# Retention in written order with lags, resident tiles refilled through their low part, and attention rows gated where they are made

## The chip, the cores and the metric

The kernel runs on one core of one Trainium2 chip. The metric is the device time of one execution in microseconds. The kernel before took 2122.32 us (median of 3 runs, 2121.36 to 2124.02). The core has five engines with a queue each: TensorE (PE in the profile, its weight loads PEld), VectorE (DVE), ScalarE (ACT), GpSimd (POOL) and SyncE (SP). In this kernel nearly all DMAs are issued by SP, one after the other.

## What is computed

One layer of a streaming encoder on 2048 rows of 1024 numbers, in float32. The rows are normalised and projected to 8192 columns, which are split into the queries, keys, values and gate of a chunked attention (8 heads of 64), the same for a retention (8 heads, keys of 64, values of 128), and two merge gates:

```python
h = rms_norm(x, norm_gain[l])
proj = jnp.einsum('bsd,df->bsf', h, w_in[l])
q_a, k_a, v_a, g_a, q_r, k_r, v_r, g_r, m_a, m_r = split_columns(proj)
o_a = chunk_band_attention(q_a, k_a, v_a, rel_bias[l])     # heads reshaped
branch_a = einsum(o_a * silu(g_a), w_out_attn[l])
o_r = retention_chunkwise(rotary(q_r), rotary(k_r), v_r, gn_gain[l])
branch_r = einsum(o_r * silu(g_r), w_out_ret[l])
mixed = sigmoid(m_a) * branch_a + sigmoid(m_r) * branch_r
x = x + einsum(mixed, w_out[l])
return rms_norm(x, final_gain)
```

Attention looks at a row's own chunk of 64 rows and the 8 before. Retention is a linear attention with a decay per head: within a block, masked scores times values; across blocks, a state of 64 x 128 per head that is carried on. Each head's output is divided by its own standard deviation (group norm), times a gain.

## The kernel before

**Numbers in two parts.** A float32 matrix is held as a high part, rounded to the type TensorE multiplies fast, and a low part, the rest. ACT makes the high part (`split`, `to_parts`: `act.copy`), DVE or POOL the low part by subtraction. A product is then three matmuls: high x high, high x low, low x high.

**The dense stream.** All large matrix products form one list, `seq`, of products in fixed order: `p0` and `g0` (projection of the first 1024 rows to queries, keys, values, then to gates), `p1` and `g1` (the same for the second 1024 rows), `ba0`, `br0`, `ba1`, `br1` (the two branch outputs of each half) and `out`. The jobs p and g run in chunks of 256 weight columns, each 7 products of Strassen's kind over 7 resident tiles `R[0..6]` (each with a high and a low part) that hold combinations of the normalised rows. The others are plain products over resident tiles that hold gated branch inputs (`ya`, `yr`) or `w_out`. One product is 12 matmuls of 512 columns in 4 steps of 3. p0, g0, p1 and g1 have 392 steps each, ba 64, br 128, out 256: 2208 steps. Weights (`raw`) are loaded one chunk ahead and made into parts 3 products ahead (`prime`, `prepare`).

**Steps as a clock of the program.** `step()` puts out one step of the stream. `later(n, fn)` puts `fn` out n steps later, `put(lag, ...)` is a store by DMA after that lag, `fill(n)` puts out n dense steps between pieces of attention or retention (fractions are kept as credit), and `limit` stops `fill` at a step. `hook` calls a function after a given product.

**Order of the queues.** TensorE and SP always run in the order in which the program is written. ACT, DVE and POOL do so while `strict[0]` is set (the projections); in attention, retention and merge a planner orders them by a model of cost. Each engine takes its queue in order, so that a waiting instruction holds those behind it.

**Stages.** p0; then `heads(0)`, which is attention of the first half with 1.0 steps of g0 at each place and retention with 2.7; p1; `heads(1)` with g1 and the first part of ba0 and br0, 1.25 and 3.3 steps; then the merge. Each stage has its pool `E` of 512-column tiles (22, 15, 21, 22 of them). Attention begins at step 412 of the stream and puts out 18 + 168 x 1.0 = 186 steps in the first half and 18 + 192 x 1.25 = 258 in the second; a retention has 12 + 69 fills.

**Retention** goes over 4 pairs of heads and 4 blocks of 256 rows (16 units), two heads each (32 items). `load` brings keys, queries, values and decayed keys of a unit (`kr`, `qr`, `vr`, `kd`) and is called some one and a half units ahead. `scores` makes `sr` in PSUM, two items ahead; DVE multiplies it by the decay mask, ACT and DVE make `sh` and `sl`. `update` makes `kv` and adds it to the state. `output` multiplies into the one PSUM bank `o`; `evacuate` copies it out (`oz`, ACT), stores it, squares it on POOL, splits the square, and one unit later `pend` sums it over rows with matmuls into `ssq`. At the end a chain of DVE instructions turns `ssq` into the reciprocal deviations `rrow`.

**Refills.** `reload` (after each product of g0's last chunk) loads the second half's combinations into tiles `hl` of `E` and splits them into `R`. `fill_ya` loads attention output and its gate, multiplies and splits; `finish_yr` (16 times in p1, 16 times in the merge) loads a head's retention output and gate, multiplies them with the gain, multiplies by the deviation, which a matmul `rb` with `rrow` spreads over partitions, and stores; `fill_yr` and `fill_wo` load and split. Line 135 of the profile is the helper that records an instruction in written order; lines 206 and 207 are `split`.

## Time and profile before

| | |
|---|---|
| median of 3 runs | 2122.32 us |
| profiled execution | 2128.98 us, span 2127.2 us |
| TensorE busy | 1972.2 us, 93%, 9744 matmuls |
| mean granted TensorE clock | 0.971 |
| attention, first and second half | from 383 to 625 us, from 1165 to 1485 us |
| retention, first and second half | from 625 to 862 us (with its chain), from 1485 to 1754 us |
| projections | from 0 to 383 us, from 862 to 1165 us |
| merge and output | from 1754 to 2127 us |

A row of waits names the instruction that waited, what released it, the total, how often and the longest. A row of a group gives line, engine, operation, output and inputs by the program's names, shape and count, then busy time, mean ns of one, and the idle time before with its releaser. A row of a tile gives least, median and greatest ns. The ends of matmuls are modelled, so that PE busy can run over short waits.

### The profile page before, as it was taken

The page shows a single profiled execution, that of the slowest core. Times are in us where ns is not written, and L with a number is a line of the kernel's source. Part 1 is how long each engine was busy: PE and PEld are TensorE (multiplying, and loading weights), DVE is VectorE, ACT ScalarE, POOL GpSimd, SP SyncE. Part 2 cuts the span into 40 slices and gives each one's busy share as a digit, 9 for nine tenths or more (in the row PEclk, how much of TensorE's full clock was granted, in tenths as well). Part 3 has the DMA queues.
Part 4 walks back from the last instruction along what each step waited for, and adds up shares of the span by engine and source line. Part 5 has one row for each costly group of instructions (what it writes and reads, how often), then busy time and mean ns, then how long its engine had stood idle before and what let it go on. Part 6 is the DMA issues. An engine that isn't in the chain of part 4 may idle for free. (4 is left out here: it accounts for less than half of the span.)

```text
span 2127.2 us, 30311 instructions
## 1 busy us (share of the span) xinstructions
PE 1972.2 (93%) x9744; PEld 1638.4 (77%) x9744; DVE 1426.2 (67%) x2491; ACT 873.3 (41%) x1727; POOL 794.2 (37%) x868
## 2 busy tenths in 40 slices
PE   5799899999999997899999999999989888999998
PEld 4677777888888886777787888888867776788886
DVE  6867777777757667778877666665665567444554
ACT  5344333556554445233334555555443230222221
POOL 2544764554433324244544544443330131021000
PEclk9899999999999998999999999999989989999999
DMA  5376786645447768566675544443879978986564
GB/s 158 91 249 180 216 274 201 203 138 154 155 139 246 232 212 275 185 222 202 201 250 185 173 153 135 147 143 100 239 245 320 296 249 317 332 294 218 192 191 142
DMA packets 335951, 438.94 MB, mean 206 GB/s; under 512 B 29976, under 2 KB 193456, under 8 KB 335792
## 3 DMA queue, kind: packets, MB, share of 16 engines
q1 hardware_dynamic: 334752, 436.99, 64.3%
q8 instruction: 78, 1.28, 0.3%
q14 instruction: 81, 0.66, 0.1%
q10 hardware_dynamic: 1040, 0.00, 0.0%
HBM read 286.13 MB, written 150.76 MB: 205 GB/s over the span
## 5 line engine op out<-in xcount | busy, mean ns | idle before, releaser
L1180 POOL TENSOR_SCALAR pr<-pr,rsum 128x640 f32<-128x640 f32 (+4 forms) x128 | 96.5, 754 | 192.9 <-DVE rsum L1179 156.1
L135 PE MATMUL ps_p_z<-r,wh_p 128*128 128x512 f32 x448 | 144.5, 404 | 13.2 <-DVE c_p L135 7.7
L135 PE MATMUL ps_p_x<-r,wh_p 128*128 128x512 f32 x448 | 145.2, 405 | 4.8 <-DVE r L135 4.7
L135 PE MATMUL ps_g_z<-r,wh_g 128*128 128x512 f32 x448 | 144.9, 405 | 1.8 <-DVE u_g L344 1.3
L135 PE MATMUL ps_g_x<-r,wh_g 128*128 128x512 f32 x448 | 146.4, 408 | 0.0
L1178 ACT ACTIVATE pr<-pr,mn 128x640 f32<-128x640 f32 (+4 forms) x128 | 97.7, 763 | 113.6 <-DVE mn L1175 113.2
L135 POOL TENSOR_TENSOR t_p<-raw_p,t_p 128x512 f32<-128x512 f32 x50 | 72.0, 1440 | 147.3 <-DVE wl_p L135 132.0
L207 DVE TENSOR_TENSOR ptl<-tp,pth 128x384 fp32r<-128x384 f32 x168 | 98.9, 598 | 34.3 <-ACT pth L206 31.8
L1065 POOL TENSOR_TENSOR gr<-gr,ta 128x512 f32<-128x512 f32 x32 | 47.1, 1473 | 194.0 <-DVE gr L1064 179.5
L1175 DVE CUSTOM_DVE_ANT_0 pr<-wide,bt 128x640 f32<-128x640 f32 (+4 forms) x128 | 94.2, 736 | 29.5 <-PE wide L135 28.2
L281 POOL TENSOR_TENSOR wl_g<-t_g,wh_g 128x512 fp32r<-128x512 f32 x52 | 67.5, 1297 | 118.2 <-ACT wh_g L280 114.3
L135 PEld LDWEIGHTS ps_p_z<-r,wh_p 128*128 128x128 f32 x448 | 84.1, 193 | 30.8 <-issue 14.4
L135 PEld LDWEIGHTS ps_p_x<-r,wh_p 128*128 128x128 f32 x448 | 85.3, 194 | 23.4 <-DVE r L135 5.7
L206 ACT CAST pth<-tp 128x384 fp32r<-128x384 f32 x168 | 84.1, 512 | 37.7 <-PE tp L135 33.1
L135 DVE TENSOR_TENSOR wl_p<-t_p,wh_p 128x512 fp32r<-128x512 f32 x108 | 98.7, 914 | 0.4 <-ACT wh_p L135 0.4
L135 PE MATMUL ps_p_x<-r,wl_p 128*128 128x512 f32 x224 | 90.2, 403 | 6.9 <-DVE wl_p L135 6.9
L1388 POOL TENSOR_TENSOR o<-oz 128x512 f32<-128x512 f32 x32 | 35.2, 1101 | 163.9 <-ACT oz L1381 142.9
L135 PEld LDWEIGHTS tp<-ident,pr 128*128 128x128 f32 x560 | 70.2, 140 | 33.8 <-DVE ptl L207 10.3
L135 PE MATMUL tp<-ident,pr 128*128 128x128 f32 x560 | 89.2, 273 | 7.0 <-DVE ptl L207 6.5
L135 PE MATMUL wide<-ka,qa 128*128 128x512 f32 (+2 forms) x448 | 93.9, 326 | 1.2 <-DVE mn L1175 1.2
L135 PE MATMUL ps_p_z<-r,wl_p 128*128 128x512 f32 x224 | 89.5, 399 | 0.4 <-DVE wl_p L135 0.4
L280 ACT CAST wh_g<-t_g 128x512 fp32r<-128x512 f32 x104 | 64.5, 621 | 61.2 <-PE ps_g_y L135 22.1
(1222 smaller groups left out, 5925.8 us busy)
## 6 DMA issues: line engine op xcount, KB each, us to landing
raw_g<-in_w_in_dram SPq DMA_DIRECT2D x56, 512.0 KB, 6.4
raw_p<-in_w_in_dram SPq DMA_DIRECT2D x52, 512.0 KB, 6.0
qa<-qas SPq DMA_DIRECT2D x128, 128.0 KB, 2.9
qr<-qrs SPq DMA_DIRECT2D x128, 128.0 KB, 3.7
vr<-vrs SPq DMA_DIRECT2D x64, 256.0 KB, 4.1
ka<-kas SPq DMA_DIRECT2D x40, 256.0 KB, 2.9
va<-vas SPq DMA_DIRECT2D x40, 256.0 KB, 3.2
kds<-kdt_k SPq DMA_DIRECT2D x32, 256.0 KB, 3.2
```

Of the source, the lines that this page charges most:

```text
L135: return tc.keep_in_program_order(op(*a, **k))
L206: act.copy(dst_h, src)
L207: (eng or dve).tensor_tensor(dst_l, src, r32(dst_h), ALU.subtract)
L280: act.copy(wh, src)
L281: soon(LO_LAG if strict[0] else 0, lambda: eng.tensor_tensor(wl, src, r32(wh), ALU.subtract))
L1065: pool.tensor_tensor(g, g, ta, ALU.add)
L1175: dve.tensor_tensor_reduce(pr[:, 0:w], sp, bts[h][:, WIN - w:WIN], 1.0, 3.0e38, ALU.add, ALU.min, mn,)
L1178: act.activation(pr[:, 0:w], pr[:, 0:w], AF.Exp, bias=mn, scale=-1.0, accum_out=rsum)
L1180: pool.tensor_scalar(pr[:, 0:w], pr[:, 0:w], rsum, 1.0, ALU.mult, ALU.mult)
L1388: pool.tensor_tensor(o2, oz, oz, ALU.mult)
```

## The change

**Retention.** All engines are put in written order after the first 12 steps (`strict[0]`), and stay so through p1. What was put out at once now has lags: scores, mask product (DVE, now into a tile `sm`), high part (ACT), low part (now POOL); `kv`, state additions, `sstk`; copy and square of `o` (the square now by ACT from PSUM), its high and low part (POOL). `sure` puts out what is deferred where an output needs it. `load` is cut in two, keys and queries two units ahead and values one unit ahead. 2.3 dense steps at each place instead of 2.7 and 3.3; attention 1.0 in both halves. In the first half `limit` keeps g0's last chunk (28 steps) out of the retention; it runs after it, with the pools of p1.

**Deviations.** The chain of 12 DVE instructions is spread over steps and its result is stored to memory (`rsscr`); `finish_yr` loads a row of it broadcast over 128 partitions and multiplies on POOL, without a matmul. In the merge the 16 calls start at step 14, every 8 steps, instead of 8 and 2.

**Refills.** `refill` loads float32 values straight into the low part of a resident tile, copies the high part from it, and subtracts in place; the lags are in steps. It stands in for tiles of `E` in `reload`, `fill_ya` and `fill_yr`; the first four calls of `fill_yr` move from ba0 to the end of g1, 14 steps apart. g0's last chunk takes its products in the order of p.

**Attention** loads the gate of a head and multiplies its output by it on POOL before storing, so that `fill_ya` loads one tile instead of two.

**Weights** are loaded 9 and 8 products before their chunk (`RAW_LEADS`) instead of 7, and in strict order the sums of the chunks of g are put out one by one. Every `E` pool has a tile more.

The diff, cut to its core:

```diff
-E_PROJ = 22
-E_ATT = 15
-E_RET = 21
-E_MRG = 22
+E_PROJ = 23
+E_ATT = 16
+E_RET = 22
+E_MRG = 23
...
-ATT_FILLS = (1.0, 1.25)
-RET_FILLS = (2.7, 3.3)
+ATT_FILLS = (1.0, 1.0)
+RET_FILLS = (2.3, 2.3)
+RAW_LEADS = (9, 8)
...
-YR_FROM = 8
-YR_EVERY = 2
+YR_FROM = 14
+YR_EVERY = 8
...
-    SUM_AT = {True: {0: ("t1", "t2"), 4: ("t3",), 2: ("t4",)}, False: {0: ("t1", "t2", "t3"), 3: ("t4",)}}
+    SUM_AT = {
+        "p": {0: ("t1", "t2"), 4: ("t3",), 2: ("t4",)},
+        "g": {0: ("t1", "t2"), 2: ("t3",), 5: ("t4",)},
+        "loose": {0: ("t1", "t2", "t3"), 3: ("t4",)},
+    }
...
-            seq = [(c, k) for c in range(n) for k in per]
+            self.orders = [name[0]] * n
+            if name == "g0":
+                self.orders[-1] = "p"
+            seq = [(c, k) for c in range(n) for k in (per if resident else ORDERS[self.orders[c]])]
...
-                if ch.job.name[0] == "p":
+                if isinstance(ch, Strassen):
                     ch.sums(k)
...
-        count = {}
+        count, begins = {}, {}
+        for at, (job, ch, n) in enumerate(seq):
+            if isinstance(ch, Strassen):
+                begins.setdefault(ch, at)
+        sooner = {at - lead: (ch, [j]) for ch, at in begins.items() for j, lead in enumerate(RAW_LEADS)}
         for at, (job, ch, n) in enumerate(seq):
             count[ch] = count.get(ch, 0) + 1
+            if at in sooner:
+                ch2, js = sooner[at]
+                if ch2.raw is None or js[0]:
+                    len(ch2.raw or ()) == js[0] and ch2.load(js)
             if count[ch] == job.when + 1 and ch in following and following[ch].raw is None:
                 following[ch].load()
...
-    def reload(m):
+    def refill(m, k, src, lag, low=None):
+        wh, wl = R[m][0][:, k, :], R[m][1][:, k, :]
+        dma(r32(wl), src)
+        later(lag, lambda: act.copy(wh, r32(wl)))
+        later(lag + 2, lambda: (low or dve).tensor_tensor(wl, r32(wl), r32(wh), ALU.subtract))
+    def reload(n):
+        m, at = PRODUCTS[n][0], ORDERS["p"].index(n)
         for k in range(4):
-            a = E(f"hl_{m}_{k}")
-            dma(a, cscr[m][k])
-            to_parts(m, k, a, pool if k == 3 else dve)
+            t = 4 * at + k
+            later(1, lambda k=k, t=t: refill(m, k, cscr[m][k], 7 + 4 * t // 3 - 4 * at, pool if t % 3 == 2 else dve))
...
     def fill_ya(s, i, m):
         for k in range(4):
-            b = 2 * s + i
-            a, u = E(f"ya_{k}_{b}"), E(f"yu_{k}_{b}")
-            dma(a, oascr[k][b])
-            dma(u, uascr[k][b])
-            (pool if k % 2 else dve).tensor_tensor(a, a, u, ALU.mult)
-            to_parts(m, k, a)
+            later(1 + k, lambda k=k: refill(m, k, oascr[k][2 * s + i], 8))
...
     def finish_yr(h, b, lead):
-        a, u = E(f"yr_{h}_{b}"), E(f"yv_{h}_{b}")
+        a, u, r = (E(f"{n}_{h}_{b}") for n in ("yr", "yv", "rb"))
         dma(a, orscr[h // 2][b][h % 2])
         dma(u, urscr[h][b])
-        row = NOH + 8 * b + h
+        dma(r, rsscr[b // 2][8 * b + h].rearrange("(o d) -> o d", o=1).broadcast_to([P, B]))
         def gated():
             dve.scalar_tensor_tensor(a, a, gn[:, h:h + 1], u, ALU.mult, ALU.mult)
         def rest():
-            rb = TR(f"rb_{h}_{b}")
-            pe.matmul(rb, ohr[:, row:row + 1].broadcast_to([P, P]), rrow, start=True, stop=True)
-            dve.tensor_tensor(a, rb, a, ALU.mult)
+            pool.tensor_tensor(a, a, r, ALU.mult)
             put(6, yrscr[h][b], a)
...
     def fill_yr(s, i, j, m):
         for k in range(4):
-            h, b = 4 * j + k, 2 * s + i
-            a = E(f"yq_{h}_{b}")
-            dma(a, yrscr[h][b])
-            to_parts(m, k, a)
+            later(1 + 2 * k, lambda k=k: refill(m, k, yrscr[4 * j + k][2 * s + i], 10))
...
     def fill_wo(i, j, m):
-        for k in range(4):
+        def fetch(k):
             a = E(f"wo_{i}_{j}_{k}")
             row = (4 * j + k) * P
             dma(a, w_out[0, row:row + P, 512 * i:512 * i + 512])
-            to_parts(m, k, a)
+            later(10, lambda: act.copy(R[m][0][:, k, :], a))
+            later(12, lambda: dve.tensor_tensor(R[m][1][:, k, :], a, r32(R[m][0][:, k, :]), ALU.subtract))
+        for k in range(4):
+            later(1 + 2 * k, lambda k=k: fetch(k))
...
                 oa = E(f"oa_{h}_{b}")[0:64]
                 act.copy(oa, po[64:128])
                 dve.tensor_tensor(oa, po[0:64], oa, ALU.add)
-                put(3, oascr[h // 2][b][64 * (h % 2):64 * (h % 2) + 64], oa)
+                pool.tensor_tensor(oa, oa, uts.pop((h, b)), ALU.mult)
+                put(6, oascr[h // 2][b][64 * (h % 2):64 * (h % 2) + 64], oa)
...
             if m < len(units):
                 prs[m].append(soft(h, b, un, 1))
+                if un == 1:
+                    load_u(h, b)
...
+        def load_valued(p, st):
+            b, un = st // 2, st % 2
+            nm = f"{p}_{st}"
+            kd = E(f"kd_{nm}", F32R, (P, 2, T))
+            dma(r32(kd), r32(kdscr[p][b][:, un]))
+            vs = []
+            for i in range(2):
...
-            dve.tensor_tensor(sp, sp, dms[p][i], ALU.mult)
-            sh = E(f"sh_{nm}", F32R)
-            sl = E(f"sl_{nm}", F32R)
-            split(sh, sl, sp)
-            return sh, sl
+            got = []
+            def masked():
+                sm = E(f"sm_{nm}")
+                dve.tensor_tensor(sm, sp, dms[p][i], ALU.mult)
+                later(2, lambda: high(sm))
+            def high(sm):
+                got.append(E(f"sh_{nm}", F32R))
+                act.copy(got[0], sm)
+                later(2, lambda: low(sm))
+            def low(sm):
+                got.append(E(f"sl_{nm}", F32R))
+                pool.tensor_tensor(got[1], sm, r32(got[0]), ALU.subtract)
+            later(1, masked)
+            return got
...
+            def added():
...
+                sstk = epool[0].tile([P, 2, DV], F32R, tag="sstk", bufs=2, name=f"sstk_{p}_{st}")
+                sstks[p, st + 1] = sstk
+                later(3, lambda: high(sstk))
+            def high(sstk):
+                act.copy(sstk[0:64], state)
+                later(1, lambda: low(sstk))
+            def low(sstk):
+                dve.tensor_tensor(sstk[64:128], state, r32(sstk[0:64]), ALU.subtract)
+                if st == 3:
...
+            later(1, added)
+        def sure(here):
+            while not here():
+                deferred.pop(0)[2]()
         def output(p, st, i, parts, ops):
-            _, qs, vs, _ = tiles[p, st]
+            qs, vs = tiles[p, st][1], values[p, st][0]
             o = ops[:, i * T:(i + 1) * T]
+            sure(lambda: len(parts) == 2 and (st == 0 or (p, st) in sstks))
...
-            oz = E(f"oz_{nm}")
-            act.copy(oz, ops)
-            put(
-                2,
-                orscr[p][b][:, :, un * T:(un + 1) * T].rearrange("i p t -> p i t"),
-                oz.rearrange("p (i t) -> p i t", i=2),
-            )
-            o2 = E(f"o2_{nm}")
-            pool.tensor_tensor(o2, oz, oz, ALU.mult)
-            oh2 = E(f"o2h_{nm}", F32R)
-            ol2 = E(f"o2l_{nm}", F32R)
-            split(oh2, ol2, o2)
+            got = []
+            def out_():
+                oz = E(f"oz_{nm}")
+                o2 = E(f"o2_{nm}")
+                act.copy(oz, ops)
+                act.activation(o2, ops, AF.Square)
+                put(
+                    2,
+                    orscr[p][b][:, :, un * T:(un + 1) * T].rearrange("i p t -> p i t"),
+                    oz.rearrange("p (i t) -> p i t", i=2),
+                )
+                later(2, lambda: high(o2))
+            def high(o2):
+                got.append(E(f"o2h_{nm}", F32R))
+                act.copy(got[0], o2)
+                later(2, lambda: low(o2))
+            def low(o2):
+                got.append(E(f"o2l_{nm}", F32R))
+                pool.tensor_tensor(got[1], o2, r32(got[0]), ALU.subtract)
+            later(1, out_)
...
-        load_masks(0)
-        load(*todo[0])
-        load(*todo[1])
+        load_scored(*todo[0])
+        load_valued(*todo[0])
+        load_scored(*todo[1])
...
         fill(12)
+        strict[0] = True
...
                 ops = ps_ret.tile([P, 512], F32, tag="o", bufs=1, name=f"o_{p}_{st}")
-            if i == 0 and st < 7:
-                update(p, st)
+                if st < 7:
+                    update(p, st)
+                if m + 1 < len(todo):
+                    load_valued(*todo[m + 1])
             fill(RET_FILL)
+            if i == 1 and pend:
+                pend()
             output(p, st, i, parts.pop((p, st, i)), ops)
-            if i == 0 and pend:
-                pend()
-                pend = None
             if i == 1:
                 pend = evacuate(p, st, ops)
...
-            if i == 1 and n + 3 < len(items):
-                p2, st2, _ = items[n + 3]
-                if st2 == 4 * s:
-                    load_masks(p2)
-                load(p2, st2)
+            if i == 0 and m + 2 < len(todo):
+                load_scored(*todo[m + 2])
             fill(RET_FILL)
         fill(RET_FILL * 2)
         pend()
...
+        chain = [
...
+        for _ in range(3):
+            chain += [
...
+        chain.append(lambda: dma(rsscr[s], y))
+        for n, fn in enumerate(chain):
+            later(1 + n, fn)
+        fill(len(chain))
...
     for n in range(7):
-        hook("g0", 13, n, lambda n=n: reload(in_resident(n)))
+        hook("g0", 13, n, lambda n=n: reload(n))
     hook("g1", 13, 0, lambda: fill_ya(0, 0, 0))
     hook("g1", 13, 1, lambda: fill_ya(0, 1, 4))
     for n, (i, j) in enumerate(RYR):
-        hook("ba0", n, 0, lambda i=i, j=j: fill_yr(0, i, j, RYR[i, j]))
+        hook("g1", 13, 6, lambda i=i, j=j, n=n: later(14 * n, lambda: fill_yr(0, i, j, RYR[i, j])))
         hook("ba1", n, 0, lambda i=i, j=j: fill_yr(1, i, j, RYR[i, j]))
...
-    limit[0] = end["g0"] + 20
+    limit[0] = end["g0"] - 28
     st = heads(0)
     limit[0] = 1 << 30
-    run_to(end["g0"])
...
     st = open_phase("proj1", E_PROJ, 4)
-    strict[0] = True
+    run_to(end["g0"])
     for n, (b, h) in enumerate((b, h) for b in range(2) for h in range(HEADS)):
         later(10 + 20 * n, lambda h=h, b=b: finish_yr(h, b, 18))
...
+    strict[0] = False
...
```

More of the change, by code (lines that the diff above doesn't have):

```diff
@@ L155, in hybrid_kernel @@
     NOH = 2 * ONE + 1
-    ohr = const.tile([P, NOH + 32], F32R, name="ohr")
+    ohr = const.tile([P, NOH], F32R, name="ohr")
     flip = const.tile([P, P], F32, name="flip")
@@ L184, in hybrid_kernel @@
     stscr = [D(f"sts_{p}", [HD, 2 * DV]) for p in range(4)]
+    rsscr = [D(f"rss_{s}", [32, B]) for s in range(2)]
     skscr = [D(f"sks_{p}", [P, 2 * DV], F32R) for p in range(4)]
@@ L323, in prepare @@
             self.sums(n)
+            for s in SUMS_OF:
+                if s[0] == PRODUCTS[n][1]:
+                    self.sum(*s)
             late = pool if n in self.job.lo_pool or self.c < self.job.front and n == 6 else dve
@@ L1273, in retention, with load_scored @@
         todo = [(p, st) for p in range(4) for st in range(4 * s, 4 * s + 4)]
-        tiles, dms = {}, {}
+        tiles, values, dms = {}, {}, {}
         begun = [False]
-        def load(p, st):
+        def load_scored(p, st):
+            if st == 4 * s:
+                load_masks(p)
             b, un = st // 2, st % 2
@@ L1316, in scores @@
             nm = f"{p}_{st}_{i}"
-            ks, qs, _, _ = tiles[p, st]
+            ks, qs = tiles[p, st]
             sp = ps_ret.tile([P, 512], F32, tag="sr", bufs=2, name=f"sr_{nm}")
@@ L1439, in retention @@
         pend()
[L1441 to L1448 removed]
+        y, tmp, hv, var = (E(f"rt{n}")[0:32] for n in range(4))
+        chain = [
+            lambda: dve.tensor_scalar(var, ssq, 1.0 / DV, GN_EPS, ALU.mult, ALU.add),
+            lambda: dve.tensor_scalar(tmp.bitcast(I32), var.bitcast(I32), 1, None, ALU.logical_shift_right),
+            lambda: dve.tensor_scalar(y.bitcast(I32), tmp.bitcast(I32), -1.0, RSQRT_MAGIC, ALU.mult, ALU.add),
+        ]
+        for _ in range(3):
+            chain += [
+                lambda: dve.scalar_tensor_tensor(tmp, y, -0.5, var, ALU.mult, ALU.mult),
+                lambda: dve.tensor_tensor(tmp, tmp, y, ALU.mult),
+                lambda: dve.scalar_tensor_tensor(y, tmp, 1.5, y, ALU.add, ALU.mult),
+            ]
+        chain.append(lambda: dma(rsscr[s], y))
+        for n, fn in enumerate(chain):
+            later(1 + n, fn)
+        fill(len(chain))
     st = open_phase("proj0", E_PROJ, 4)
@@ L1495, in hybrid_kernel @@
     ahead[0] = AHEAD
-    pool.memset(r32(rrow), 0.0)
     def tables_():
-        oh = E("oh", shape=(P, NOH + 32))
+        oh = E("oh", shape=(P, NOH))
         ext = E("ext", shape=(HEADS, 257))
         held = E("held", shape=(HEADS, 511))
-        dma(oh, onehot[:, 0:NOH + 32])
+        dma(oh, onehot[:, 0:NOH])
         dma(ext, rel_rev)
```

63 lines of the change are left out of this document (26 added, 37 removed).

## The prediction

> **What bounds the kernel now.** I read the page's totals first, then the busy time of each engine in one stretch for each stage, then the waits of TensorE in those stretches, and a timeline around the longest wait.
>
> ```profile
> span 2127.2 us, 30311 instructions
> PE 1972.2 (93%) x9744; PEld 1638.4 (77%) x9744; DVE 1426.2 (67%) x2491; ACT 873.3 (41%) x1727; POOL 794.2 (37%) x868
> ```
>
> TensorE is the bound on the average, and no other engine is near it. Its clock matters too, so I count as the loss of a stretch its length minus (PE busy x granted clock). The columns are the stretch, its length, the busy time of PE, PEld, DVE, ACT and POOL with instructions, the granted clock, the DMA share and GB/s:
>
> ```profile
> 45.00:383.00 338.00, 305.92 (x1376) 247.60 (x1377) 256.11 (x336) 138.15 (x270) 190.18 (x135) 0.96 0.63 200
> 383.00:625.00 242.00, 234.66 (x1323) 198.56 (x1322) 172.49 (x375) 140.76 (x308) 119.75 (x222) 1.00 0.50 153
> 625.00:862.00 237.00, 210.88 (x1112) 179.51 (x1110) 163.73 (x274) 105.46 (x200) 82.55 (x63) 0.94 0.73 230
> 862.00:1165.00 303.00, 290.85 (x1302) 236.41 (x1303) 228.71 (x321) 108.23 (x203) 136.33 (x96) 0.98 0.66 214
> 1165.00:1485.00 320.00, 313.03 (x1768) 264.87 (x1767) 210.20 (x423) 179.49 (x363) 152.82 (x267) 1.00 0.46 142
> 1485.00:1754.00 269.00, 236.58 (x1216) 200.94 (x1215) 169.38 (x274) 95.89 (x173) 65.78 (x50) 0.92 0.84 270
> 1754.00:1830.00 76.00, 66.40 (x278) 52.45 (x277) 50.53 (x73) 7.09 (x13) 13.44 (x9) 0.98 0.89 320
> 625.00:740.00 115.00, 108.66 (x594) 93.25 (x593) 75.70 (x132) 50.96 (x97) 39.38 (x32) 0.99 0.80 246
> ```
>
> Losses: first projection 44.3 us, attention 7.3 and 7.0, second projection 18.0, start of the merge 10.9. The two retentions lose most: 237 - 210.88 x 0.94 = 38.8, and 269 - 236.58 x 0.92 = 51.3, together 90 us. The first 115 us of retention 0, before any refill, lose only 115 - 108.66 x 0.99 = 7.4 (6.4%). What TensorE waits for, first in retention 0, then in retention 1 (total, times, longest):
>
> ```profile
> PE sr L135 <- DMA qr<-qrs: 8.4, 5, 3.3
> PE o L135 <- ACT oz L1381: 7.2, 2, 4.4
> PE ssq L135 <- ACT o2h L206: 2.5, 2, 1.4
> PE ssq L135 <- DVE o2l L207: 1.8, 2, 1.1
> ...
> PE o L135 <- ACT oz L1381: 16.6, 2, 9.1
> PE sr L135 <- DMA qr<-qrs: 9.9, 4, 5.8
> PE ssq L135 <- DVE o2l L207: 3.8, 5, 1.2
> ```
>
> The longest one in the timeline:
>
> ```profile
> 1583.88 1.14 ACT L206 CAST r<-ya 128x512 fp32r<-128x512 f32 x2 [1.78 <-DVE ya L1006]
> ...
> 1589.21 0.58 ACT L1381 COPY oz<-o 128x512 f32<-128x512 f32 x1
> 1589.84 0.80 PE L135 MATMUL o<-qr,sstk 128*128 128x256 f32 x2 [9.07 <-ACT oz L1381]
> ```
>
> The copy that empties the only `o` bank stands on ScalarE behind the casts of a refill (`r<-ya`). So TensorE pays for the order on another queue, not for too little work there: ACT is busy 36% of that stretch.
>
> **The dense step as the unit.** A step is three matmuls of 512 columns:
>
> ```profile
> 1830.58 2.72 PE ps_ba_(1, 0)_19111 L135 x12
> ```
>
> Twelve take 2.72 us, so a step takes 0.68 us. The number of dense steps does not change; fills of 2.3 and 1.0 only move 40 steps out of retention 0 (69 x 0.4 = 28 by the fills, 12 that ran beyond g0), 56 net out of retention 1 and 48 out of attention 1, to stages where they cost the same. A move is worth nothing by itself. What counts is the losses and the matmuls that go.
>
> **Removed matmuls.** 32 broadcasts of the deviation:
>
> ```profile
> L135 PE MATMUL rb<-rrow,ohr x32: 392/397/632, 878.2 to 1798.0; 128*128 128x512 f32 x32
> ```
>
> 512 columns each, 2.72/12 = 0.227 us at the dense rate: **-7.3 us**, all on the bound engine. Their product moves from DVE (0.68 us) to POOL. Its price there is that of `gr<-gr,ta`, the same shape from SBUF:
>
> ```profile
> L1065 POOL TENSOR_TENSOR gr<-gr,ta 128x512 f32<-128x512 f32 x32 | 47.1, 1473 | 194.0 <-DVE gr L1064 179.5
> fg<-in_final_gain_dram SPq DMA_DIRECT2D x32, 256.0 KB, 5.6
> ```
>
> 16 x 1.47 = 24 us of POOL in the second projection, where it is busy 136 of 303; hidden there, and 24 us if that cover went. The broadcast load has a like one in `fg`, 5.6 us to landing, against 18 steps (12 us) of lead: hidden; in the merge the lead is 8 steps (5.4 us), so it may be late by a fraction, off TensorE's queue. Attention's 32 gating products on POOL (at most 1.47 us each, at least nothing; half that rows, I take 1) lie in a POOL that is half idle: 0.
>
> **Retention in written order.** Own TensorE work of a retention: 128 `sr`, 240 to 256 `o`, 48 to 64 `kv` and 64 `ssq` matmuls of 256 columns, 496 by the loops; at half of 0.227 us that is 56 us (an estimate). Dense steps: retention 0 begins at step 412 + 186 = 598 and stops at 784 - 28 = 756, so 158 x 0.68 = 107; retention 1 has 12 + 69 x 2.3 + 13 = 184, so 125. Without loss 163 and 181 us. What share is lost? Below, the 6.4% of the stretch without refills; above, the 90/506 = 18% of now. The `oz` and `ssq` waits come from the order that the change replaces (lags of 1 to 2 steps, refills with lags of 7 to 10); the `qr` waits (18.3 of 53.6 us named, with the smaller ones) come from late loads, which are issued in the same order as before and have less dense time over them. I take 9%, nearer to the quiet stretch: 163 x 0.09/0.91 = 16 and 18 us, so 90 - 34 = **-56 us**.
>
> The engines change load with it:
>
> ```profile
> L207 DVE TENSOR_TENSOR sl<-sr,sh 128x512 fp32r<-128x512 f32 x32 | 21.9, 687 | 11.0 <-ACT sh L206 10.2 <-DMA ors<-oz 0.7
> L1388 POOL TENSOR_TENSOR o<-oz 128x512 f32<-128x512 f32 x16 | 17.5, 1093 | 105.0 <-ACT oz L1381 84.1 <-DMA yq<-yrs 16.1 <-issue 4.8
> ```
>
> 96 subtractions (64 `sl`, 32 `o2l`) leave DVE, 66 us over both stages, and cost POOL 96 x 1.29 = 124 (the `wl_g` row below) less 32 x 1.1 = 35 for the squares, which ACT does for about 19. All three stay under 75% of 340 us (DVE: 164 + 169 now, less 66, less some 50 of refills that leave these stages), so this is nothing unless POOL fails (a rival below). The value loads go one unit ahead and the score loads two, past each other on SP only; one tile more in each pool fits that. The store of a gated attention tile waits three steps more and is read tens of steps later.
>
> DMA does not forbid it:
>
> ```profile
> q1 hardware_dynamic: 38540, 54.34, 72.8%
> hl<-cs SPq DMA_DIRECT2D x28, 256.0 KB, 5.3
> ```
>
> In retention 0, 54.3 MB took 0.728 x 237 = 172.5 us of queue time. Without the 7 MB of `hl` and some 2.9 MB of 40 dense steps, 141 us remain for 163 to 180: 79 to 86%, against 80% in the quiet stretch.
>
> **The end of retention 0 and the refill.** This costs. The limit leaves 12.7 fill steps and the 13 of the chain without dense cover: the last unit goes `o`, copy, square, cast, POOL subtraction, `ssq` with TensorE idle.
>
> ```profile
> L1381 ACT COPY oz<-o x32: 569/587/589, 647.0 to 1746.1; 128x512 f32<-128x512 f32 x32
> L281 POOL TENSOR_TENSOR wl_g<-t_g,wh_g 128x512 fp32r<-128x512 f32 x12 | 15.5, 1291 | 51.9 <-ACT wh_g L280 51.9
> L201 DVE TENSOR_TENSOR rt<-rt,rt x6: 678/679/681, 854.7 to 1762.0; 32x512 f32<-32x512 f32 x6
> L207 DVE TENSOR_TENSOR r<-hl,r x21: 675/684/1684, 810.2 to 848.0; 128x512 fp32r<-128x512 f32 x21
> SPq L135 <- DVE rrow L1445: 16.2, 1, 16.2
> ```
>
> 3 x 0.59 + 1.29 = 3.1 us, about 4 with the unit before; in retention 1 each idle us came with 18.9/32.4 = 0.58 us lost to the clock, so 6. Then twelve chain instructions of 0.68 us hold DVE 8 us, and the store of the result holds SP behind it (the row before shows SP behind such a chain for 16.2 us), so the first refill loads leave about 6 us late. In the 52 steps (35 us) until the last resident tile is wanted, DVE has 8 + 19 x 0.68 to 1.1 for low parts + some 20 of dense work = 41 to 49 us. Its excess of 6 to 14 us falls on TensorE where the seven products queue; I take 8. Together **+14** (0 if the 56 us of order gains hide it, 26 at worst).
>
> **The rest.** Merge: the waits `rb<-rrow` 3.6 and `rb<-yr` 4.7 lose their instruction, and 16 finishes spread over 128 steps instead of 32 in a stretch whose DMA share is 0.89: 10.9 to 5, **-6**. Earlier weight loads: the waits on `wl_p` that they could cure total
>
> ```profile
> PE ps_p_x L135 <- DVE wl_p L135: 6.9, 5, 2.6
> L135 DVE TENSOR_TENSOR wl_p<-raw_p,wh_p x76: 675/684/1779, 89.0 to 1144.4; 128x512 fp32r<-128x512 f32 x76
> ```
>
> Some of these are DVE's own queue, so **-3** (0 to -10). Attention 1 with thinner cover: the share lost with fills of 1.0 in attention 0 is 3.0% against 2.2%, so **+1**.
>
> Sum: -7.3 - 56 + 14 - 6 - 3 + 1 = -57. The profiled execution took 2128.98 us (span 2127.2), 0.3% above the median 2122.32 of the runs; I take the sum off the median: **2065 us**.
>
> **A rule that speaks against it.** The row above shows `wl_p` at 684 ns mostly and 1779 at worst, a POOL instruction's length more. The Trainium skill, SBUF — State Buffer, section "Who interferes with whom", has it that a DVE instruction with two SBUF inputs and a GpSimd one that reads SBUF shut each other out for the whole instruction; the trace agrees. By that rule up to 96 subtractions moved to POOL could each hold one weight split on DVE; the sum would stay as long as both queues have slack, and go to the POOL rival below if not.
>
> **Rivals.**
> - *POOL becomes the bound of retention: slower.* In written order `sl` waits behind the dense sums on POOL:
>
> ```profile
> L313 POOL TENSOR_TENSOR t_g<-raw_g 128x512 f32<-128x512 f32 x3 | 3.9, 1285 | 15.1 <-DMA raw_g<-in_w_in_dram 15.1
> L207 POOL TENSOR_TENSOR r<-hl,r 128x512 fp32r<-128x512 f32 x7 | 11.9, 1694 | 18.9 <-ACT r L206 15.1 <-DVE r L207 3.8
> ```
>
> A sum waits 5 us for its weights in retention 1, then two sums and `sl` at 1.69: 10 us. Scores lead outputs by 9.2 steps, of which the lags use 5; the other 4.2 are 5 us. So TensorE would lose 5 x 1.58 = 8 us for each of the 342/28 = 12 chunks: 96, hence 2161. It decides once weights come 5 us late and POOL runs at 1.69. Against it: the earlier loads and 63% POOL load at 1.3 us (12 x 7.9 + 96 x 1.3 = 220 of 352).
> - *Loads stay late.* The `qr` share, 18.3/53.6 of 90 = 31 us, stays and doubles as the stage gets denser: gain 28 instead of 56, **2093**. For it: 79 to 86% DMA share.
> - *The refill by way of the low part starts too late.* It cannot load before TensorE has left the tile, where `hl` could: 26 at the first end and 10 at the four tiles of ba1, **2087** or, if DVE holds both, 2100.
> - *It all comes out.* Retention at attention's 3% (11 us lost), the end hidden for 5: **2030**.
>
> **How the numbers follow.** Forecast 0.52, late loads 0.14, late refill 0.11, all out 0.07, POOL 0.16. A measurement of this kernel tells about 0.2% (4 us) from no change. No difference gets 0.05, three parts of it from the refill, two from POOL; faster 0.52 + 0.14 + 0.08 + 0.07 = 0.81, slower 0.14. The range 2030 to 2118 holds all but the POOL case and the worst of the refill; the forecast alone spans 2045 to 2085 (retention at 6.4 to 12%: -10, +13; the end at 4 to 21: -10, +7).
>
> **What would show it.** Retention stretches of about 180 and 200 us at clocks above 0.97; no `o` wait on `oz` above 1 us; `qr` waits at half or less; an idle TensorE of some 4 us before the last `ssq` of retention 0 and waits on `r` after it. I am wrong if POOL `sl` ends late for TensorE, if DMA share passes 0.9 in retention, or if the second projection loses over 35 us.

## The result and the profile after

The changed kernel takes 2048.91 us (median of 4 runs, 2046.29 to 2053.57) against 2121.84 us for the kernel before beside it: a ratio of 0.9658, 95% interval 0.9636 to 0.9679, 73 us less. Forecast were 2065 us and a range of 2030 to 2118. The gain is larger than the 57 us that the steps add up to, and it lies in fewer places than they said.

The page of the changed kernel, its totals:

```profile
span 2045.2 us, 30554 instructions
PE 1939.0 (95%) x9712; PEld 1611.5 (79%) x9712; DVE 1359.5 (66%) x2347; ACT 888.5 (43%) x1759; POOL 966.9 (47%) x989
```

32 matmuls are gone, POOL has 173 us more and DVE 67 us less. The stretches of the changed kernel, columns as in the prediction (first projection, attention 0, retention 0, its end and the refill, second projection, attention 1, retention 1, merge):

```profile
45.00:376.00 331.00, 302.14 (x1377) 243.71 (x1376) 254.76 (x336) 137.57 (x269) 190.87 (x135) 0.97 0.64 203
376.00:623.00 247.00, 233.99 (x1314) 197.16 (x1313) 168.68 (x374) 140.75 (x308) 140.87 (x236) 1.00 0.52 157
623.00:789.00 166.00, 163.89 (x945) 142.60 (x944) 96.19 (x176) 85.84 (x166) 101.42 (x79) 1.00 0.88 266
789.00:845.00 56.00, 46.96 (x196) 35.52 (x195) 51.07 (x58) 29.78 (x56) 31.13 (x21) 0.97 0.67 230
845.00:1140.00 295.00, 281.58 (x1275) 230.36 (x1274) 228.03 (x296) 105.94 (x199) 165.68 (x114) 0.98 0.72 228
1140.00:1425.00 285.00, 277.13 (x1601) 234.02 (x1600) 196.51 (x404) 166.11 (x339) 154.13 (x269) 1.00 0.52 157
1425.00:1604.00 179.00, 178.02 (x1019) 154.91 (x1019) 106.96 (x175) 94.48 (x174) 104.97 (x78) 1.00 0.88 269
1604.00:1750.00 146.00, 143.04 (x625) 116.58 (x624) 81.05 (x118) 30.18 (x51) 43.11 (x32) 1.00 1.01 367
```

Read as losses (length minus busy time x clock), beside the kernel before and the forecast:

| stretch | loss before | forecast | loss after |
|---|---|---|---|
| first projection | 44.3 | about 42 | 37.9 |
| attention 0 | 7.3 | 7 | 13.0 |
| retention 0 | 38.8 with its end | 16 | 2.1 |
| end of retention 0, refill | (in the row above) | 14 | 10.4 |
| second projection | 18.0 | about 17 | 19.0 |
| attention 1 | 7.0 | 8 | 7.9 |
| retention 1 | 51.3 | 18 | 1.0 |
| start of the merge | 10.9 | 5 | 3.0 |

The two retentions fall from 90 us to 3, with 10 more for the end of the first. TensorE has nothing left to wait for in them; these are all its waits, in retention 0 and in retention 1:

```profile
PE kv L136 <- DMA vr<-vrs: 1.4, 2, 0.9
PE sr L136 <- DMA qr<-qrs: 0.7, 1, 0.7
...
PE sr L136 <- DMA qr<-qrs: 1.0, 1, 1.0
```

TensorE's own work in them came out as forecast (163.9 and 178.0 us busy, against 163 and 181). The clock is 1.00 in both, where it was 0.94 and 0.92: the second part of what a wait cost. With the 7.3 us of the matmuls removed the table's differences come to some 90 us; the span of the profiled executions fell by 82, the median by 73. A clock printed to 0.01 is worth 3 us in a stretch of 300, so no row of the long stretches is good to better than that.

### The profile page after: what moved, and what is told of

It reads as the page before. It is cut to its first block, busy times and chain, and to the rows that moved or that the text cites. A ratio compares the mean times of both kernels' runs of the same rounds, so it can differ in the third digit from the quotient of the medians.

```text
span 2045.2 us, 30554 instructions
## 1 busy us (share of the span) xinstructions
PE 1939.0 (95%) x9712; PEld 1611.5 (79%) x9712; DVE 1359.5 (66%) x2347; ACT 888.5 (43%) x1759; POOL 966.9 (47%) x989
## 5 line engine op out<-in xcount | busy, mean ns | idle before, releaser
L136 POOL TENSOR_TENSOR sl<-sm,sh 128x512 fp32r<-128x512 f32 x64 | 87.1, 1361 | 59.5 <-ACT sh L136 52.8
L136 DVE TENSOR_TENSOR wl_p<-t_p,wh_p 128x512 fp32r<-128x512 f32 x112 | 112.5, 1005 | 0.4 <-ACT wh_p L136 0.4
L208 ACT CAST pth<-tp 128x384 fp32r<-128x384 f32 x168 | 84.2, 513 | 38.8 <-PE tp L136 32.6
L136 PE MATMUL ps_g_x<-r,wl_g 128*128 128x512 f32 x224 | 88.6, 395 | 2.3 <-DVE wl_g L136 2.3
L136 PEld LDWEIGHTS wide<-ka,qa 128*128 128x128 f32 x448 | 76.0, 188 | 18.2 <-DVE mn L1200 5.8
L136 DVE TENSOR_TENSOR sm<-sr,dm 128x512 f32<-128x512 f32 x64 | 44.2, 690 | 68.9 <-PE sr L136 43.1
```

Source lines behind the costliest of these rows:

```text
L136: return tc.keep_in_program_order(op(*a, **k))
L208: act.copy(dst_h, src)
```

## The experiments

Each edit is to the changed kernel unless it says otherwise. The time of a version is the median of 4 runs, the ratio is to the kernel before on the same chip. Two versions whose intervals overlap are not told apart by their times; there the stretches of the profile decide, as far as they can.

**Order by the planner again.** `strict[0] = True` moves from the retention to the second projection:

```diff
         fill(12)
-        strict[0] = True
         parts = {items[0]: scores(*items[0])}
...
     st = open_phase("proj1", E_PROJ, 4)
+    strict[0] = True
     run_to(end["g0"])
```

> The changed kernel, with ACT, DVE and POOL left to the planner in the retentions (the lags, the refills, the loads and the fills stay). Theory A, the written order took the stalls away: the o bank waits for its copy and ssq for its parts again, both retentions lose 20 us or more each, time 2085 to 2110. Rival B, the bursts of refills were the cause and they are gone from the retentions anyway: the retentions lose less than 8 us each, time 2045 to 2060.

2096.0 us, ratio 0.9879 (0.985 to 0.9908): 47 us of the 73 are lost. The two retentions of this version:

```profile
623.00:812.00 189.00, 171.71 (x946) 146.58 (x946) 98.60 (x176) 88.60 (x167) 101.34 (x78) 0.97 0.76 234
1449.00:1652.00 203.00, 185.93 (x1013) 157.34 (x1012) 102.89 (x177) 94.86 (x173) 104.29 (x78) 0.97 0.77 234
```

and the waits of TensorE in the second of them:

```profile
PE o L136 <- POOL sl L1378: 8.1, 11, 1.7
PE ssq L136 <- POOL o2l L1468: 5.1, 4, 3.0
PE o L136 <- ACT o L1453: 3.3, 3, 1.4
PE sr L136 <- DMA qr<-qrs: 0.6, 1, 0.6
```

They lose 22 and 23 us (189 - 171.71 x 0.97, 203 - 185.93 x 0.97) with about the same work on each engine, and TensorE waits in them only for instructions and loads of the retention itself. What these stand behind shows in the timeline around one of the waits (ACT, POOL, then PE):

```profile
1478.06 0.62 ACT L1373 CAST sh<-sm 128x512 fp32r<-128x512 f32 x1
...
1479.53 1.27 POOL L319 TENSOR_TENSOR t_g<-raw_g,raw_g 128x512 f32<-128x512 f32 x1
1480.76 1.26 POOL L1378 TENSOR_TENSOR sl<-sm,sh 128x512 fp32r<-128x512 f32 x1
...
1482.07 0.38 PE L136 MATMUL o<-sl,vr 128*128 128x256 f32 x1 [1.74 <-POOL sl L1378]
```

`sh` is ready at 1478.7 us, but POOL does a sum of dense weights (`t_g`) before it subtracts `sl` from it, and TensorE waits for that. Theory A holds: what this flag switches is worth 47 us. One thing stays open: the flag sets more than the order of the queues. While it is on, the low part of a dense weight is put out 4 steps after its high part (`LO_LAG`), and the weight sums are spread wider; this run lost that too in the retentions, and the two were not taken apart.

It is not all of the gain. With the 11 us of the end of retention 0 this version loses 56 us where the kernel before lost 90, so 34 us went without the written order. No `o` wait is longer than 2.5 us here, against 9.1 before, and the `qr` waits stay away.

**Written order without lags inside the chains.** All nine lags of `scores`, `update` and `evacuate` become 0, so that the links stand behind each other one step after their matmuls:

```diff
-                later(2, lambda: high(sm))
+                later(0, lambda: high(sm))
...
-            later(1, masked)
+            later(0, masked)
...
```

> The changed kernel in written order, but the lags inside the retention chains taken out: mask product, high part and low part stand one behind the other, one step after their matmuls (the same for the state and the square). Theory A1, the lags carry the gain as much as the order, since an instruction that waits for the one before it on another engine holds its own queue: loss of 10 to 25 us in each retention, time 2065 to 2100. Rival A2, the order of the queues is enough, since scores lead outputs by two items: time within 6 us of 2049.

2048.39 us, ratio 0.9655 (0.9627 to 0.9683): nothing lost, A2 holds. The two retentions:

```profile
623.00:791.00 168.00, 166.14 (x960) 144.72 (x959) 102.90 (x177) 88.08 (x168) 104.47 (x79) 1.00 0.85 263
1428.00:1607.00 179.00, 178.20 (x1020) 155.06 (x1020) 101.11 (x176) 95.42 (x174) 102.65 (x78) 1.00 0.87 270
```

Scores are made two items ahead of their output; that distance hides the chain whether its links are spread or not.

**One part alone, in the kernel before: ACT in written order in the retentions**, DVE and POOL by the planner:

```diff
+    act_strict = [False]
+    class ActOrdered(Ordered):
+        def __getattr__(self, name):
+            return super().__getattr__(name) if strict[0] or act_strict[0] else getattr(self.engine, name)
...
         fill(12)
+        act_strict[0] = True
         parts = {items[0]: scores(*items[0])}
...
+        act_strict[0] = False
```

> The kernel before with one part of the change alone: in the retentions ACT is in written order, DVE and POOL stay with the planner; loads, refills and fills as before. Theory M, the copy of the o bank standing behind refill casts on ACT was the main cost, so that the 23.8 us of waits of o for oz go, with the clock that they cost: time 2085 to 2105. Rival N, the order must hold on all three engines, else the wait moves to DVE and POOL, or ACT in written order stands still where the tiles of a refill land late: 2110 or more.

2149.25 us, ratio 1.0131 (1.0113 to 1.0148): slower than the kernel before, by 1.3%. Rival N. TensorE's waits for the copy of `o` grow from 23.8 to 30.4 us, the longest to 12.8, and ACT now stands in turn (waits of TensorE in the whole run, then waits of ACT from 1485 to 1790 us):

```profile
PE o L135 <- ACT oz L135: 30.4, 6, 12.8
PE ssq L135 <- ACT o2h L135: 16.5, 9, 3.4
...
ACT sstk L135 <- DVE state L1359: 39.4, 6, 11.9
ACT r L135 <- DVE ya L1012: 37.8, 8, 10.0
ACT o2h L135 <- POOL o L1394: 28.4, 16, 4.0
ACT r L135 <- DMA yq<-yrs: 26.5, 8, 9.4
```

A written order on one engine made it wait for engines that the planner had ordered otherwise, and for refill tiles that landed late. So the order did not pay on ACT alone; whether it needs all three engines, or refills whose casts come after their data, was not tried in the kernel before. How the 26 us beyond the 47 divide between refills, loads and matmuls is not shown.

**Loads of a unit joined again**, one and a half units ahead:

```diff
+        load_valued(*todo[1])
...
-                if m + 1 < len(todo):
-                    load_valued(*todo[m + 1])
...
-            if i == 0 and m + 2 < len(todo):
+            if i == 1 and m + 2 < len(todo):
                 load_scored(*todo[m + 2])
+                load_valued(*todo[m + 2])
```

> The changed kernel with the loads of a unit joined again and issued one and a half units ahead, as before. Theory C, the waits for qr (18.3 us before, 1.7 us now) went because the loads were cut in two, so that fewer tiles are held and SP waits less for a free one: qr waits of 8 us or more return, time 2060 to 2085. Rival D, qr was late because SP stood behind stalled engines, whose tiles came free late: qr waits stay under 4 us, time within 5 us of 2049.

2055.35 us, ratio 0.9691 (0.9656 to 0.9725): not told apart from the changed kernel by its time, which lies between the two theories. The waits of TensorE for `qr`, in the whole run and in the stretch from 1425 to 1610 us:

```profile
PE sr L136 <- DMA qr<-qrs: 5.6, 6, 1.6
...
PE sr L136 <- DMA qr<-qrs: 3.3, 4, 1.6
```

5.6 us lies between them too: neither C's 8 nor D's under 4. Cutting the loads is worth some 4 us of waits. The planner's order left them at 1.5 us in the whole run, and refills through tiles (below) at 1.8, so neither the written order nor the refills without tiles alone removed the rest of the 18.3; what did is open.

**Low parts on DVE.** `sl` and `o2l` subtract there instead of on POOL:

```diff
-                pool.tensor_tensor(got[1], sm, r32(got[0]), ALU.subtract)
+                dve.tensor_tensor(got[1], sm, r32(got[0]), ALU.subtract)
...
-                pool.tensor_tensor(got[1], o2, r32(got[0]), ALU.subtract)
+                dve.tensor_tensor(got[1], o2, r32(got[0]), ALU.subtract)
```

> The changed kernel with the low parts sl and o2l on DVE instead of POOL. Theory I, both queues have slack in the retentions, so that it does not matter which takes 96 subtractions: time within 6 us of 2049. Rival J, POOL and DVE hold each other up (tensor_tensor at 1.7 us instead of 0.7 or 1.3), and the POOL copies cost the retentions or spare them time: a change of more than 8 us, either way.

2050.71 us, ratio 0.9666 (0.9647 to 0.9686): nothing. In the retentions

```profile
623.00:791.00 168.00, 164.98 (x950) 143.41 (x948) 122.88 (x222) 87.03 (x168) 44.31 (x32) 1.00 0.87 263
1427.00:1606.00 179.00, 177.02 (x1014) 153.89 (x1013) 132.44 (x222) 92.83 (x173) 43.71 (x30) 1.00 0.88 267
```

POOL falls from 105 to 44 us in the second, DVE rises from 107 to 132 of 179, and TensorE is as busy as with them on POOL. Theory I: both queues have room.

**Attention's gating on DVE:**

```diff
-                pool.tensor_tensor(oa, oa, uts.pop((h, b)), ALU.mult)
+                dve.tensor_tensor(oa, oa, uts.pop((h, b)), ALU.mult)
```

> The changed kernel with the 32 gating products of attention on DVE instead of POOL. Theory E, the first attention lost 5 us because zeroing instructions (pth, ptl) and normalisations stand behind the gating on POOL: the wait of po for the POOL zeroing (4.7 us) goes, that attention loses 8 us instead of 13, time 2040 to 2045. Rival F, it comes of other parts (earlier weight loads, another tile in the pool): the wait stays, time 2046 to 2053.

2042.72 us, ratio 0.9628 (0.9594 to 0.9662), the fastest of all, though its interval overlaps that of the changed kernel. TensorE's waits for the zeroing on POOL in attention 0 with the change, and with this edit; and POOL's price for the gating in the changed kernel:

```profile
PE po L136 <- POOL pth L1230: 4.7, 4, 1.8
```

```profile
PE po L136 <- POOL pth L1230: 2.9, 2, 1.8
```

```profile
L1256 POOL TENSOR_TENSOR oa<-oa,ua x32: 1278/1287/1297, 408.5 to 1427.2; 64x512 f32<-64x512 f32 x32
```

Attention 0, from its first score to the first score of the retention, takes 239 us with the change (391.0 to 630.0) and 236 here (389.6 to 625.7); before it was 231 (398.3 to 629.7). So by one profile of each some 3 of the 8 us lost are the gating on POOL, in front of instructions that write zeros for TensorE; the other 5 stay, with 2.9 us of the same wait. Theory E in its direction, not in its size.

**No early weight loads**, on top of the version with the gating on DVE: the table `sooner` is left empty, so that weights load 7 products ahead.

```diff
-        sooner = {at - lead: (ch, [j]) for ch, at in begins.items() for j, lead in enumerate(RAW_LEADS)}
+        sooner = {}
```

> The version with the gating on DVE (2042.7 us) without the early weight loads (7 products ahead again). Theory T, as the prediction had it, early loads spare the projections some 3 us: time 2043 to 2050. Rival U, they are what still holds attention 0 above its old length (236.1 us against 231.4 from its first score to the retention's first): without them it falls to 233 or less, and the time to 2040 or less.

2046.39 us, ratio 0.9633 (0.9619 to 0.9648), against 2042.72: not told apart. The 3.7 us fit theory T and are no more than its runs differ by. The profiles do not settle it: attention 0 begins at 394.9 us here, and between 389.6 and 395.6 in those with early loads. Attention 0 takes 235 us, not 233, so U has no support. TensorE does not wait for the zeroing there at all in this version, so that wait is not what keeps the stage above 231 us; what does is open.

**More cover at the end of retention 0**, 12 steps more before the limit:

```diff
-    limit[0] = end["g0"] - 28
+    limit[0] = end["g0"] - 16
```

> The changed kernel with 12 more dense steps allowed in retention 0 (the limit is 16 steps before the end of g0 instead of 28), so that its last units have cover. Theory K, the idle 3.1 us before the last ssq and a part of the waits for wl_g and r after it come of the missing cover: time 2042 to 2047. Rival L, the end is bound by DVE (chain, low parts of the refill), which has the same work in the same time: within 3 us of 2049, the wait only moves.

2051.58 us, ratio 0.9661 (0.9631 to 0.9692): no gain that the times tell (its four runs lie between 2041.8 and 2054.59), as rival L has it. The waits of TensorE between 789 and 845 us in the changed kernel, largest first, and between 785 and 850 us here:

```profile
PE ps_g_x L136 <- DVE wl_g L136: 2.3, 1, 2.3
PE ssq L136 <- ACT o2h L136: 2.0, 1, 2.0
PE ps_p_x L136 <- DVE wl_p L136: 1.2, 1, 1.2
PE ssq L136 <- POOL o2l L136: 1.1, 1, 1.1
```

```profile
PE ps_g_z L136 <- DVE c_g L136: 9.8, 1, 9.8
```

The waits for `ssq` are gone, and one of 9.8 us for DVE has come, as much as all waits of that stretch in the changed kernel (9.1 us with the smaller ones): `c_g` stands on DVE behind the chain and low parts of the refill (the chain begins at 804.6 us, `c_g` at 821.6). DVE is the bound of that stretch, 51 of 56 us busy in the changed kernel.

**Refills through tiles**, at the same steps and with the same lags:

```diff
-        dma(r32(wl), src)
-        later(lag, lambda: act.copy(wh, r32(wl)))
-        later(lag + 2, lambda: (low or dve).tensor_tensor(wl, r32(wl), r32(wh), ALU.subtract))
+        a = E(f"rf_{m}_{k}")
+        dma(a, src)
+        later(lag, lambda: act.copy(wh, a))
+        later(lag + 2, lambda: (low or dve).tensor_tensor(wl, a, r32(wh), ALU.subtract))
```

> The changed kernel with the refills loaded into tiles of the pool and split from there, at the same steps and with the same lags. Theory V, the way by the low part costs nothing, since its loads have 7 to 10 steps of lag and the waits of TensorE for refilled tiles total 2.5 us between 789 and 845: time within 4 us of 2049. Rival W, the low part can be loaded only after TensorE has left the tile, and that is late: 5 us or more faster with tiles. Rival X, the tiles bind the pool, SP stands on free ones and loads come late: 5 us or more slower.

2053.57 us, ratio 0.9671 (0.9656 to 0.9685). W is out: loading into the resident tile itself is not late. V and X are not told apart, nor is this version from the changed kernel; if there is a cost of tiles, it is the 4.7 us between the medians.

**The second half nearly as thin as before** (thin: more dense steps at each place, so that the stage is longer; 3.1 in its retention, where the kernel before had 3.3), with the finishes of the merge close, since I expected them after their readers otherwise:

```diff
-ATT_FILLS = (1.0, 1.0)
-RET_FILLS = (2.3, 2.3)
+ATT_FILLS = (1.0, 1.25)
+RET_FILLS = (2.3, 3.1)
...
-YR_FROM = 14
-YR_EVERY = 8
+YR_FROM = 8
+YR_EVERY = 2
```

> The changed kernel with the second half as thinly packed as before: 1.25 steps at each place of attention 1, 3.1 in retention 1, and the finishes of the merge from step 8, every 2 (else they would come after their readers). Theory G, moving dense steps is worth nothing by itself: time within 8 us of 2049, the two stages longer and the merge shorter by the same. Rival H, the denser packing is a part of the gain: 15 us or more lost, time over 2064.

2087.03 us, ratio 0.9842 (0.982 to 0.9864): 38 us lost. Theory G falls. The waits of TensorE in retention 1 (1456 to 1695 us), then in the merge:

```profile
PE o L136 <- ACT o L136: 11.6, 2, 7.4
PE sr L136 <- DMA qr<-qrs: 2.6, 3, 1.6
...
PE ps_ba_(0, 0)_19011 L136 <- ACT wh_ba_(0, 0)_18954 L282: 22.4, 1, 22.4
```

The cast of those weights was waiting for its load:

```profile
1765.15 0.62 ACT L282 CAST wh_ba_(0, 0)_18954<-raw_ba 128x512 fp32r<-128x512 f32 x1 [43.08 <-DMA raw_ba<-in_w_out_attn_dram]
```

Two more runs take this apart. **Close finishes alone** (`YR_FROM = 8`, `YR_EVERY = 2` in the changed kernel):

> The changed kernel with the finishes of the merge as close as before: from step 8, every 2 steps. Theory O, as the prediction had it, spreading them spares the merge some 6 us: time 2052 to 2058. Rival P, the finishes fill the DMA queue ahead of the weights of the next job, as in the run with thin fills, where TensorE waited 22.4 us for wh_ba behind them: 15 us or more lost, time over 2063. Rival Q, with the chain spread over steps and no matmul the finishes hinder nobody: within 3 us of 2049.

2072.43 us, ratio 0.9769 (0.9746 to 0.9792): rival P, 23.5 us lost. The first 96 us of the merge, the longest waits of TensorE in them, and what the cast of the first of these weights waited for:

```profile
1604.00:1700.00 96.00, 72.67 (x296) 58.14 (x295) 52.90 (x80) 17.11 (x29) 26.17 (x20) 0.89 1.01 368
```

```profile
PE ps_br_(0, 0)_18388 L136 <- ACT wh_br_(0, 0)_18281 L282: 9.9, 1, 9.9
PE ps_br_(0, 0)_18559 L136 <- ACT wh_br_(0, 0)_18493 L282: 7.2, 1, 7.2
PE ps_ba_(0, 0)_18248 L136 <- ACT wh_ba_(0, 0)_18134 L282: 5.0, 1, 5.0
```

```profile
1658.75 0.62 ACT L282 CAST wh_br_(0, 0)_18281<-raw_br 128x512 fp32r<-128x512 f32 x1 [23.10 <-DMA raw_br<-in_w_out_ret_dram]
```

Sixteen finishes with three loads and a store each fill the DMA engines (share 1.01 in both cases, 367 GB/s when they are spread); close together they stand in front of the weights. **Retention 1 thin, finishes every 5 steps** (`RET_FILLS = (2.3, 3.1)`, `YR_FROM = 8`, `YR_EVERY = 5`):

> The changed kernel with only retention 1 thin (3.1 steps at each place), attention 1 as changed, the finishes of the merge from step 8, every 5. Theory R, the loss of 38 us with thin fills has two causes, and one of them is in the retention: where it runs over ba0 and br0, its o bank waits on ACT behind their work (11.6 us in that run), so 10 to 20 us remain here: time 2059 to 2069. Rival S, it was the close finishes in the merge alone: time within 6 us of 2049.

2057.0 us, ratio 0.969 (0.9671 to 0.971): 8 us between the medians, which overlapping intervals do not tell from nothing, below R's range and above S's. In its profile `o` waits 2.2 us for ACT and TensorE 6.3 us for `wh_br` in the merge. So of the 38 us some 23 are what the close finishes cost by themselves, and the thin retention is worth 8 at most. Some 7 are left: the thinner attention 1, which was not tried alone, or the parts together.

## Why the prediction was right, step by step

- **Removed matmuls, -7.3 us.** They went, and their products on POOL and loads held TensorE up nowhere: none of its waits names `rb` or `yr`. The 7.3 itself was not measured apart.
- **Retention in written order, -56 us.** The mechanism was right, and it is the term that was mis-sized: its loss was forecast at 9%, and 2.1 of 166 and 1.0 of 179 us are about 1%. That is 31 us more gain than the 56. The step that failed is the one that left the waits for late `qr` loads where they were, because loads were "issued in the same order as before and have less dense time over them". They fell from 18.3 to 1.7 us while the DMA share rose to 0.88, above the 79 to 86% worked out. The quiet stretch of 6.4% (625 to 740 us before), taken as the floor, was none, and for the same reason: its waits were mostly for those loads.

```profile
PE sr L135 <- DMA qr<-qrs: 5.2, 4, 2.0
PE o L135 <- DVE sl L207: 1.2, 1, 1.2
```

And the gain was put on lags and order together. The lags inside the chains are worth nothing; the written order, with the dense weights' own lags that hang on the same flag, is worth 47 us; 34 us of the 90 went without it, and no run shows by which part of the change.
- **A moved step is worth nothing.** Not so for the packing of the second half. Putting it back cost 38 us, most of it by the finishes of the merge, which stood close with it; the thin retention with looser finishes cost 8 at most, so the rule is not refuted for the steps themselves. The term of -6 for the merge came out at -8, but spreading the finishes was worth 23.5 us in the changed kernel.
- **The end of retention 0, +14.** 10.4 measured, 9.1 of it waits: 3.1 for `ssq` and 6.0 for weights and refilled tiles, where 8 was taken. The idle time before the last `ssq` was 3.1 us as worked out (2.0 + 1.1), and DVE was the bound, as said; more cover did not help, as that implies. One link was half wrong: the first refill loads did not leave late. Nine were issued from 795.1 us, ahead of the chain's store; SP waited for the chain only after them, 6.7 us, and the other 19 left from 808.1 us on.
- **Attention, +1.** Too small: +5.7 in attention 0, whose fills did not change, and +0.9 in attention 1. I had called the 32 gating products hidden because POOL is half idle. Some 3 us of the loss are theirs, as far as one profile tells: POOL also writes zeros for TensorE there, and 1.29 us in front of that is late. The rest is open.
- **Early weights, -3.** Within what the runs differ by; neither shown nor excluded.
- **POOL as the bound**, the slower rival, had no part: POOL was busy 206 of 345 us in the retentions, about the 63% worked out, and with 61 us less on it in retention 1 nothing moved. The Trainium skill's rule from SBUF — State Buffer, "Who interferes with whom", is seen at work elsewhere, in the chain after retention 0, where DVE instructions with two SBUF inputs take 1.67 instead of 0.68 us while POOL subtracts (the lines are at the end). **Loads stay late** had the right sign only where the loads were joined again (4 us of waits), **late refill** none, and **it all comes out** was right for the retentions, not for their end.

## What to carry to other kernels

When the bound engine waits for a copy on an engine that is a third busy, read what stands in front of that copy on its queue: a written order on all engines that share the chain was worth 47 us here (with the lags of the dense weights that came with it), and on one of them alone, in the kernel before, it cost 26. An engine that is half idle is no cover for an instruction that someone waits behind. Bursts of loads are to be spread where weights pass the same queue: 16 finishes closer together cost 23 us at the same number of bytes.

## What was not expected of the hardware

A DMA share of 0.88 over 170 us, and of 1.01 over the first 146 us of the merge, went with waits of TensorE of 1 to 3 us in each stretch. With the finishes close together the same share of 1.01 went with 22 us of waits for weights. So the share did not tell late data here; what stood in the queue ahead of the weights did. A POOL product of 64 x 512 took 1.29 us, as long as its subtractions of 128 x 512 (1.29 to 1.30 at the median): half the partitions saved nothing. In the chain of twelve DVE instructions after retention 0, three took some 1.67 us instead of 0.68 and two more some 1.4, so it lasted 12.9 us (794.7 to 807.6) and not the 8 that were worked out. The slow three, a quick one after them, and what POOL did meanwhile:

```profile
801.16 1.67 DVE L136 TENSOR_TENSOR rt<-rt,rt 32x512 f32<-32x512 f32 x1
802.86 3.37 DVE L136 SCALAR_TENSOR_TENSOR rt<-rt,rt 32x512 f32<-32x512 f32 x2
806.26 0.68 DVE L136 TENSOR_TENSOR rt<-rt,rt 32x512 f32<-32x512 f32 x1
...
800.66 1.62 POOL L136 TENSOR_TENSOR wl_g<-t_g,wh_g 128x512 fp32r<-128x512 f32 x1 [2.68 <-ACT wh_g L136]
802.36 1.62 POOL L136 TENSOR_TENSOR t_p<-raw_p,raw_p 128x512 f32<-128x512 f32 x1
803.95 1.73 POOL L136 TENSOR_TENSOR r<-r,r 128x512 fp32r<-128x512 f32 x1
```
